# A two-layer hybrid trunk on one core: the projection tiles of a head pair are spread differently over its twelve slots

## The chip, the cores and the metric

The kernel runs on one core of a Trainium2 chip. The metric is the device time of one launch in microseconds. Three timed runs of the kernel before gave 2581.28, 2585.04 and 2586.94 us, so the median is 2585.04 us.

## The reference

The reference is a trunk of two layers over 256 context tokens and 512 latent tokens, with a model width of 1024. Each layer modulates a normalised input with a shift and a scale that come from a conditioning vector, runs a mixer, and then runs a squared-ReLU feed-forward block. The mixer of layer 0 is a gated delta rule, and that of layer 1 is retention. Only layer 0's mixer is touched by the change:

```python
proj = concat([hc, hl]) @ w_in                  # q, k, v, gate z, and the decays
qkv  = silu(short_conv(qkv, conv_w))
q, k = l2norm(q) * d ** -0.5, l2norm(k)
g, beta = -exp(a_log) * softplus(a + dt_bias), sigmoid(b)
o = bidirectional_prefix_scan(q, k, v, g, beta, n_ctx)   # chunks, both directions
y = (rmsnorm(o, norm_g) * silu(z)) @ w_out
```

Within a chunk the scan solves a unit triangular system made of `k k^T`, the decays and `beta`; from chunk to chunk it carries a state of 128 by 128 per head:

```python
sol = triangular_solve(a + eye, rhs)
un  = u - w @ s
o   = qd @ s + qk @ un
s   = s * gt + kd^T @ un
```

The modulation vectors come from `silu(c) @ w_mod + b_mod` for the latent and the context vector.

## The kernel before

Layer 0's mixer has 16 value heads in 8 pairs; the two heads of a pair share one query and one key head. Tokens are cut into 6 chunks of 128. `layer0_mix` (L289) first normalises the tokens, then prepares pair 0, and then enters a loop over pairs `p` and, in each pair, over twelve slots `n`. What runs in a slot is written out by hand:

- **The chain.** Each slot calls `gdn_step` (L826) once: six chunks, two directions in turn. A step multiplies the state by key and query (L847, L848), lets VectorE form the right-hand side `r` (L851), multiplies it by the inverse (L865), lets ACT scale and copy the result (L870, L873), updates the state (L875, L882) and forms the output (L886, L892). The step of one direction needs the state that the last step of that direction left.
- **The projection tiles.** A tile is one `conv_tile` (L572) or `z_tile` (L437). It loads 128 columns of the input weight in two halves (SP's queue, L72), splits each half into a high and a low part (ACT L56, VectorE L57), and runs two groups of 24 matmuls in L91: `gl` for the latent tokens (512 columns) and `gc` for the context (256 columns). Both land in PSUM under one tag with two buffers. A conv tile is emptied by an ACT copy (L579) and three VectorE passes per group (L582), and then gets its SiLU on ACT (L592 key, L595 query, L629 value). A gate tile is emptied by ACT alone (L442) and is stored to DRAM (L443). A pair has five tiles: key and query for pair `p + 2` (generator `g1`, from `gdn_s1`, whose third step forms the norms, L604), two value tiles for pair `p + 1` (`gv`, from `gdn_sv`), and one gate tile (`fill_z`).
- **The decays.** `gdn_bt` (L632) loads rows of cumulative decay and runs 24 ReLUs (L649) and 24 exponentials (L657) on ACT. `gdn_s2` (L661) multiplies them on VectorE with key-key and key-query products from TensorE (L670; L673, L679, L682), transposes blocks (L691), sends small blocks through DRAM (L695, L705), and runs 60 short VectorE instructions of a substitution on them (L717, L720).
- **The inverse.** `gdn_iv` (L725) sends the result through DRAM (L734, L742, L743), transposes blocks (L745, L747) and puts the inverse of each chunk together in steps of small matmuls with evictions between them (L754 to L805).
- **Modulation rows.** `mod_rows` (L220) computes 128 columns of a later modulation vector: two loads on SP's queue (L224, L226), matmuls into a PSUM buffer with the tag `py` (L232), four VectorE adds (L236) and a store (L237). The same tag serves the key and value transposes that a chain starts with (`gdn_kn`, L809, at slots 9 and 10 of the pair before; L816, L822).

The framework's scheduler turns this into one order per engine. Work in a `high_priority` block is treated as if it stood that many instructions earlier: the chain 300 (`PRI`), decays, substitution, inverse and outputs 400 (`P2`), key and query tiles 250 (`PS`). Value and gate tiles and modulation rows have no such block, so they stand where the loop puts them and fill what the rest leaves. On the chip every engine follows its order, and an instruction that waits holds up those behind it on its engine.

After the loop the remaining gate tiles run, then the output projection (`out0`), the feed-forward block, layer 1 and its feed-forward block.

Of the kernel before, what the change touches and what calls it, by code (L numbers as in the profile page):

```python
# [29 lines left out]
PRI = 300  # L30
PS = 250
P2 = 400
ZN = (6,)
GATE = 4
G3 = {11: 4}
SC0 = (3, 4)
# [6 lines left out]
class Trunk:  # L43
# [245 lines left out]
    def layer0_mix(self):  # L289
        nc = self.nc  # L290
        es_a = ExitStack()
        es_b = ExitStack()
        self.psg = self.pool(es_a, "psg", space=PSUM)
        self.gc = ("gl", 2)
        psk = self.pool(es_a, "psk", space=PSUM)
        self.wraw = self.pool(es_a, "wraw0", bufs=2)
        self.whl = self.pool(es_a, "whl0", bufs=3)
        keep = self.pool(es_a, "keep")
        with ExitStack() as es:
            npool = self.pool(es, "n0", bufs=2)  # L300
            mpool = self.pool(es, "m0")
            wpool = self.pool(es, "m1")
            col = self.mod_start(mpool, psk, "kk0")
            raw = mpool.tile([128, 8, T], F32, name="xraw")

            def x_tile(t):
                x = npool.tile([128, D], F32, tag="x0", name="x0", bufs=3)
                nc.sync.dma_start(out=x, in_=self.src_x(t))
                r, xn = self.norm_stat(npool, x)
                nc.vector.tensor_scalar(out=xn, in0=x, scalar1=r, scalar2=None, op0=ALU.mult)  # L310
                for half in range(2):
                    ps = psk.tile([128, 4, 128], F32, tag=("uo0", "uo1")[half], name="nps")
                    for k in range(4):
                        nc.tensor.transpose(ps[:, k, :], xn[:, (half * 4 + k) * 128:(half * 4 + k + 1) * 128], self.ident)
                    dst = raw[:, half * 4:half * 4 + 4, t * 128:(t + 1) * 128]
                    if half:
                        nc.scalar.activation(out=dst, in_=ps, func=AF.Copy)
                    else:
                        nc.vector.tensor_copy(dst, ps)

            mods = self.mod_cols(wpool, psk, ("kk0", "kk1"), col, raw)
            for ts in ORDER0:
                next(mods)
                for t in ts:
                    x_tile(t)
            for _ in mods:
                pass
        self.gdn_globals(keep, psk)
        self.gdn_buffers(keep)
        scan = self.pool(es_a, "scan")  # L330
        prep = self.pool(es_b, "prep")
        self.yd = self.dram.tile([16, 128, T], F32, name="yd")
        self.zd = self.dram.tile([16, 128, T], F32, name="zd")
        zs = iter(range(16))

        def fill_z():
            h = next(zs, None)
            if h is not None:
                self.z_tile(h, prep)

        st = [{} for _ in range(8)]
        self.mark = {}
        free = ("kk0", "kk1", "uo0", "uo1")
        s1 = [self.gdn_s1(p, st[p], psk, scan, prep) for p in range(8)]
        sv = [self.gdn_sv(p, st[p], prep) for p in range(8)]
        s2 = [self.gdn_s2(p, st[p], psk, scan, prep, free if p == 0 else ("pp",) if p == 1 else ("kk0", "kk1", "uo0")) for p in range(8)]
        hi = lambda: self.tc.high_priority(PRI)
        for _ in s1[0]:
            pass
        self.gdn_bt(0, st[0], prep)  # L350
        n = 0
        while True:
            with hi():
                if next(s2[0], 0) == 0:
                    for _ in self.gdn_iv(0, st[0], psk, prep, free):
                        pass
                    self.gdn_kn(0, st[0], psk, scan)
                    self.gdn_kn(1, st[0], psk, scan)
                    self.gdn_bt(1, st[1], prep)
                    break  # L360
            if n == 0:
                fill_z()
            if n in (5, 6):
                next(sv[0])
            elif 7 <= n < 10:
                next(s1[1], None)
            elif n >= 12 and n % 2 == 0 and n < 26:
                fill_z()
            n += 1
        es_l = ExitStack()  # L370

        mods = [
            self.mod_rows(prep, psk, "py", 0, ch, q) for ch in (2, 3, 4) for q in range(8)]
        mods = itertools.chain(*mods)
        ys = []
        for p in range(8):
            g1 = s1[p + 2] if p < 6 else iter(())
            gv = sv[p + 1] if p < 7 else iter(())
            g2 = s2[p + 1] if p < 7 else iter(())
            for n in range(12):  # L380
                with hi():
                    self.gdn_step(p, n // 2, n % 2, st[p], psk, scan)
                with self.tc.high_priority(P2):
                    if n == 1:
                        self.gdn_kn(2, st[p], psk, scan)
                    while ys and ys[0][0] <= 12 * p + n:
                        _, q, k = ys.pop(0)
                        self.gdn_y2(q, k, st[q], psk, self.mark["DVE"])
                    for k, last in enumerate((1, 4, 5)):
                        if n == 2 * last + 1:  # L390
                            self.gdn_y(p, k, st[p], psk, scan, scan)
                            ys.append((12 * p + n + YD, p, k))
                    for _ in range(4 if n < GATE else 0):
                        next(g2, None)
                    if n == GATE and p < 7:
                        for _ in g2:
                            pass
                        for _ in self.gdn_iv(p + 1, st[p + 1], psk, prep, gate=self.mark["ACT"]):
                            pass
                    if n in (9, 10) and p < 7:  # L400
                        self.gdn_kn(n - 9, st[p + 1], psk, scan)
                    if n in G3 and p < 6:
                        for _ in range(G3[n]):
                            next(s2[p + 2], None)
                if p < 7:
                    if n in (3, 5):
                        next(gv, None)
                    with self.tc.high_priority(PS):
                        if n in (0, 2, 4):
                            next(g1, None)  # L410
                        if n == 6 and p < 6:
                            self.gdn_bt(p + 2, st[p + 2], prep)
                    if n in ZN or (n == 9 and p == 6):
                        fill_z()
                    if n in (4, 5, 6) or n == 3 and p < 4:
                        next(mods, None)
                elif n == 1:
                    es_b.close()
                    prep = self.pool(es_l, "last")
                elif n % 3 == 0:  # L420
                    fill_z()
        with hi():
            for _, q, k in ys:
                self.gdn_y2(q, k, st[q], psk, None)
        for _ in range(16):
            fill_z()
        es_l.close()
        self.es_gdn = es_a
# [949 lines left out]
```

## Time and profile before

| | us |
|---|---|
| median of three runs | 2585.04 |
| the profiled execution | 2573.84 |
| its span, first to last instruction | 2572.1 |
| TensorE busy in the span | 2431.1 |
| chains of pairs 0 to 7, from the first step at about 188 to about | 932 |
| end of pair 0, 1, 2, 3 | 256, 373, 486, 583 |
| end of pair 4, 5, 6, 7 | 685, 785, 873, 932 |

A pair ends where the last output matmul of its chain (L886) starts. The profile is one execution with a time for every instruction. In a timeline row stand the start, the length, the engine, the line, the operation, output and inputs, the count, and in brackets the idle time of that engine just before, with the instruction that ended it. TensorE's weight loads (PEld) overlap its matmuls (PE). The granted clock is the share of TensorE's full speed; 1.00 is full speed. A matmul with float32 operands leaves two records.

### The profile page before, as it was taken

The page shows a single profiled execution, that of the slowest core. Times are in us where ns is not written, and L with a number is a line of the kernel's source. Part 1 is how long each engine was busy: PE and PEld are TensorE (multiplying, and loading weights), DVE is VectorE, ACT ScalarE, POOL GpSimd, SP SyncE. Part 2 cuts the span into 40 slices and gives each one's busy share as a digit, 9 for nine tenths or more (in the row PEclk, how much of TensorE's full clock was granted, in tenths as well). Part 3 has the DMA queues.
Part 4 walks back from the last instruction along what each step waited for, and adds up shares of the span by engine and source line. Part 5 has one row for each costly group of instructions (what it writes and reads, how often), then busy time and mean ns, then how long its engine had stood idle before and what let it go on. Part 6 is the DMA issues. An engine that isn't in the chain of part 4 may idle for free.

```text
span 2572.1 us, 39043 instructions
## 1 busy us (share of the span) xinstructions
PE 2431.1 (95%) x14879; PEld 2008.7 (78%) x14879; DVE 1667.7 (65%) x3362; ACT 1073.5 (42%) x2357; POOL 221.7 (9%) x268
## 2 busy tenths in 40 slices
PE   8799798998898999999999998999999999999998
PEld 4687686786777788778888887878888887788887
DVE  5568767787776755887776668874353546644446
ACT  5575555574555553253222221653231322532222
POOL 1102111111101110200000002000000002000001
PEclk9899899999899999999999999999999999999999
DMA  6332423423232247354443444243132223432332
GB/s 214 89 96 73 110 63 97 113 72 101 69 87 72 73 145 229 122 180 127 139 143 119 130 132 124 84 134 94 50 83 61 78 66 113 148 100 90 107 90 90
DMA packets 346827, 276.94 MB, mean 108 GB/s; under 512 B 105608, under 2 KB 293488, under 8 KB 346640
## 3 DMA queue, kind: packets, MB, share of 16 engines
q1 hardware_dynamic: 345616, 271.30, 35.4%
q10 hardware_dynamic: 1024, 3.15, 0.5%
q8 instruction: 117, 1.92, 0.3%
q14 instruction: 70, 0.57, 0.1%
HBM read 241.72 MB, written 32.67 MB: 107 GB/s over the span
## 4 chain that ended last, share of the span: by engine, by line
PE 55%; DVE 7%; DMA 3%; issue 2%; ACT 2%; POOL 0%; SPq 0%; POOLq 0%; ACTq 0%; DVEq 0%
PE pn L940 21%; PE gl L91 13%; PE rvp L1257 5%; PE gc L91 3%; PE rl L91 3%; PE rgp L1257 3%; PE pv L1287 2%; PE sc L1265 1%; DVE hl L57 1%; DVE ma L199 1%; PE rc L91 1%; DMA mraw<-in_w_mod 1%; ACT hl L56 0%; DVE o0acc L976 0%; DMA raw<-in_gdn_w_out 0%
## 5 line engine op out<-in xcount | busy, mean ns | idle before, releaser
L91 PE MATMUL gl<-xt,hl 128*128 128x512 f32 (+2 forms) x2760 | 700.8, 403 | 51.7 <-DVE acc L582 31.6
L91 PEld LDWEIGHTS gl<-xt,hl 128*128 128x128 f32 x2760 | 514.9, 193 | 160.0 <-issue 27.3
L57 DVE TENSOR_TENSOR hl<-raw,hl 128x1024 fp32r<-128x1024 f32 (+1 forms) x306 | 329.2, 1078 | 226.7 <-ACT hl L56 225.6
L940 PE MATMUL pn<-hl,fh 128*128 128x512 f32 x1920 | 445.0, 391 | 2.0 <-DVE fh L1074 1.9
L56 ACT ACTIVATE hl<-raw 128x1024 fp32r<-128x1024 f32 (+1 forms) x306 | 280.1, 920 | 396.9 <-PE pn L940 263.0
L940 PEld LDWEIGHTS pn<-hl,fh 128*128 128x128 f32 x1920 | 357.1, 188 | 80.1 <-DVE fh L1074 5.1
L91 PE MATMUL gc<-xt,hl 128*128 128x256 f32 x1944 | 274.8, 290 | 9.4 <-DVE acc L582 4.7
L91 PEld LDWEIGHTS gc<-xt,hl 128*128 128x128 f32 x1944 | 254.4, 194 | 20.6 <-ACT zs L442 5.4
L199 DVE SCALAR_TENSOR_TENSOR ma<-mraw,cst,ma 128x256 f32<-128x256 f32 x280 | 127.6, 496 | 40.0 <-DMA mraw<-in_w_mod 37.7
L940 PE MATMUL pn<-hl,yh 128*128 128x512 f32 x576 | 137.4, 397 | 5.4 <-DVE yh L57 4.1
L954 DVE TENSOR_TENSOR facc<-pn,facc 128x512 f32<-128x512 f32 x120 | 82.5, 689 | 83.1 <-PE pn L940 82.7
L1257 PE MATMUL rvp<-hl,xt 128*128 128x512 f32 x576 | 133.3, 390 | 0.6 <-DVE hl L57 0.6
L940 PEld LDWEIGHTS pn<-hl,yh 128*128 128x128 f32 x576 | 108.4, 191 | 31.2 <-DVE yh L57 5.8
L1257 PEld LDWEIGHTS rvp<-hl,xt 128*128 128x128 f32 x576 | 107.7, 188 | 23.5 <-DVE hl L57 1.1
L1071 ACT ACTIVATE fr<-gl 128x512 f32<-128x512 f32 x64 | 38.2, 597 | 202.1 <-PE gl L91 202.1
L582 DVE SCALAR_TENSOR_TENSOR acc<-gl,cw,acc 128x511 f32<-128x511 f32 (+1 forms) x96 | 71.5, 745 | 39.3 <-ACT acc L579 38.5
L977 POOL TENSOR_TENSOR facc<-facc,rx 128x1024 f32<-128x1024 f32 x10 | 26.5, 2645 | 781.1 <-DVE facc L976 478.8
L940 PE MATMUL pn<-hl,ryt 128*128 128x512 f32 x384 | 91.7, 396 | 0.0
L1257 PE MATMUL rgp<-hl,xt 128*128 128x512 f32 x384 | 91.3, 393 | 0.0
L91 PE MATMUL rl<-xt,hl 128*128 128x512 f32 x384 | 89.5, 391 | 0.4 <-DVE hl L57 0.4
L717 DVE TENSOR_TENSOR tmp<-u 112x30 f32<-112x30 f32 (+14 forms) x240 | 81.3, 339 | 9.2 <-POOL u L709 6.0
L940 PEld LDWEIGHTS pn<-hl,ryt 128*128 128x128 f32 x384 | 71.5, 187 | 17.0
(282 smaller groups left out, 3437.0 us busy)
## 6 DMA issues: line engine op xcount, KB each, us to landing
raw<-in_w_ff SPq DMA_DIRECT2D x128, 512.0 KB
mraw<-in_w_mod SPq DMA_DIRECT2D x112, 256.0 KB
raw<-in_gdn_w_in SPq DMA_DIRECT2D x96, 256.0 KB
raw<-in_ret_w_in SPq DMA_DIRECT2D x32, 512.0 KB
mraw<-in_w_mod SPq DMA_DIRECT2D x24, 512.0 KB
e<-gd SPq DMA_DIRECT2D x32, 384.0 KB
mraw<-in_w_mod SPq DMA_DIRECT2D x8, 1024.0 KB
raw<-in_gdn_w_out SPq DMA_DIRECT2D x16, 512.0 KB
```

Source lines behind the costliest of these rows:

```text
L56: nc.scalar.activation(out=hi, in_=src, func=AF.Copy)
L57: nc.vector.tensor_tensor(out=lo, in0=src, in1=hi.bitcast(F32), op=ALU.subtract)
L91: nc.tensor.matmul(ps, lhsT=w(a, k), rhs=xt[:, b, k, t0:t0 + n], start=(k == 0 and i == 0), stop=(k == 7 and i == 2))
L199: eng.scalar_tensor_tensor(out=accs[v], in0=raw[:, k], scalar=c, in1=accs[v], op0=ALU.mult, op1=ALU.add)
L582: nc.vector.scalar_tensor_tensor(out=acc[:, t0 + a:t0 + a + m], in0=ps[:, b:b + m], scalar=c[j], in1=acc[:, t0 + a:t0 + a + m], op0=ALU.mu ...
L717: nc.vector.tensor_tensor(out=t3, in0=u3[:, 0:c, c:c + 1].to_broadcast([112, c, n]), in1=u3[:, c:c + 1, c + 1:32].to_broadcast([112, c, n] ...
L940: m = nc.tensor.matmul(ps, lhsT=lhs(a, k, t), rhs=hls[hf][k // 2][:, b, k % 2], start=(k == 0 and n == 0), stop=(k == 3 and n == 2))
L954: nc.vector.tensor_tensor(out=dst, in0=ps, in1=dst, op=ALU.add)
L977: nc.gpsimd.tensor_tensor(out=a, in0=a, in1=x, op=ALU.add)
L1071: nc.scalar.activation(out=r, in_=ps, func=AF.Relu)
L1257: nc.tensor.matmul(ps, lhsT=xt[:, a, kk, t * 128:(t + 1) * 128], rhs=hls[kk // 2][:, b, kk % 2], start=(kk == 0 and n == 0), stop=(kk == 7 ...
L1287: nc.tensor.matmul(pvs[it], lhsT=pts[jt][:, i, it * 128:(it + 1) * 128], rhs=v[:, j, jt], start=(jt == 0 and n == 0), stop=(jt == 5 and n ...
```

## The change

The slots of a pair are dealt out differently. The two value tiles move from slots 3 and 5 to 4 and 6. The gate tile moves from slot 6 to 10. The modulation rows move from slots 4, 5 and 6 to 5, 7 and 8; the one at slot 3 in the first four pairs stays. Key and query tiles (slots 0 and 2), norms (slot 4), decays (slot 6), the second gate tile of pair 6 (slot 9), the chain and its priorities stay.

```diff
-ZN = (6,)
+ZN = (10,)
...
                 if p < 7:
-                    if n in (3, 5):
+                    if n in (4, 6):
                         next(gv, None)
                     with self.tc.high_priority(PS):
                         if n in (0, 2, 4):
                             next(g1, None)
                         if n == 6 and p < 6:
                             self.gdn_bt(p + 2, st[p + 2], prep)
                     if n in ZN or (n == 9 and p == 6):
                         fill_z()
-                    if n in (4, 5, 6) or n == 3 and p < 4:
+                    if n in (5, 7, 8) or n == 3 and p < 4:
                         next(mods, None)
```

The scheduler answers with another order on every engine. Three places of it, first boundary between pairs on TensorE, the second on ACT, and the one between pairs 4 and 5 on TensorE, are shown in the prediction.

## The prediction

> **What bounds the kernel now.** The page comes first. TensorE is busy nearly all the time, so a pure change of order can win only where TensorE waits.
>
> ```profile
> span 2572.1 us, 39043 instructions
> PE 2431.1 (95%) x14879; PEld 2008.7 (78%) x14879; DVE 1667.7 (65%) x3362; ACT 1073.5 (42%) x2357; POOL 221.7 (9%) x268
> ```
>
> The change concerns the pair loop alone. Second view: busy time by stretch. Seven stretches run from the last step of one pair's chain to the first steps of the next (I call them seams 1 to 7, seam 1 lying between pairs 0 and 1); the last row is the loop from seam 1 to the end of pair 7. Columns: length, then PE, PEld, DVE, ACT, POOL busy, then the granted clock, the share and the GB/s of DMA.
>
> ```profile
> 256.00:320.00 64.00, 50.99 (x589) 42.82 (x590) 48.00 (x113) 33.99 (x85) 7.84 (x14) 0.84 0.40 106
> 373.00:427.00 54.00, 43.81 (x287) 36.73 (x287) 36.80 (x85) 31.27 (x76) 8.17 (x14) 0.94 0.42 115
> 484.00:530.00 46.00, 40.25 (x318) 33.55 (x315) 35.06 (x86) 21.45 (x62) 6.49 (x9) 1.00 0.44 123
> 575.00:628.00 53.00, 41.50 (x349) 34.43 (x337) 39.01 (x93) 25.00 (x62) 7.19 (x10) 0.90 0.41 108
> 684.00:723.00 39.00, 26.54 (x190) 21.00 (x187) 31.33 (x78) 15.69 (x38) 5.47 (x8) 0.87 0.45 119
> 785.00:830.00 45.00, 36.77 (x247) 30.27 (x245) 30.98 (x73) 22.97 (x49) 8.52 (x15) 0.92 0.34 89
> 866.00:900.00 34.00, 33.62 (x512) 27.24 (x511) 19.71 (x45) 15.96 (x42) 2.57 (x3) 1.00 0.31 86
> 256.00:932.00 676.00, 602.80 (x5749) 501.42 (x5749) 497.22 (x1297) 387.14 (x1115) 102.27 (x147) 0.95 0.31 83
> ```
>
> Length less PE gives the idle time: 13.0, 10.2, 5.75, 11.5, 12.5, 8.2 and 0.4 us, 61.5 of the loop's 73.2. So the chains are packed and the seams are not. Third view, who TensorE waited for from 256 to 940 us (total, times, longest):
>
> ```profile
> PE gl L91 <- DVE acc L582: 23.9, 6, 9.1
> PE gl L91 <- DVE hl L57: 6.8, 4, 3.1
> PE ivps L754 <- DVE v L745: 6.0, 1, 6.0
> PE gl L91 <- ACT hl L56: 4.7, 2, 4.3
> PE mps L232 <- DVE mrow L236: 3.9, 1, 3.9
> ```
>
> Projection tiles share two PSUM banks (tag gl, two buffers), and a value tile frees a bank only after an ACT copy (L579) and three VectorE passes (L582). At a seam ACT also owes 24 exponentials (L657) and VectorE the decay products (L673 to L682) for the next pair. Seam 2 shows the queueing: the copy stood behind all 24.
>
> ```profile
> 382.94 7.13 ACT L657 ACTIVATE e<-e,lw 128x128 f32<-128x128 f32 x24
> 385.13 3.03 PE L91 MATMUL gc<-xt,hl 128*128 128x256 f32 x24
> 388.10 0.62 PE L232 MATMUL mps<-mraw,cst 128*2 128x128 f32 x16
> 390.09 1.28 ACT L629 ACT_TABLE_LOAD   x1
> 392.13 0.67 ACT L579 ACTIVATE acc<-gl,cw 128x512 f32<-128x512 f32 x1
> 397.78 4.76 PE L91 MATMUL gl<-xt,hl 128*128 128x512 f32 x14 [9.06 <-DVE acc L582]
> ```
>
> **The change part by part.** Nothing is added to or taken from the arithmetic: five tiles and three or four modulation rows per pair, as before. The one new instruction is an activation table load (45 against 44 in the order), on ACT, which is busy 16 to 34 of the 39 to 64 us of a seam; other ACT idle time hides it, and I cost it at nothing; without that cover it costs its own 1.3 us (the row at 390.09 above). What changes is which work meets which seam.
>
> Seam 1. Before, TensorE ran out of tiles while the inverse's blocks made their trip through DRAM; then the inverse ran bare and at a slow clock.
>
> ```profile
> 257.20 1.50 PE L604 MATMUL ssps<-ones,sq 128*128 128x1 f32 x12
> 261.31 5.78 PE L91 MATMUL gl<-xt,hl 128*128 128x512 f32 x24
> 273.94 1.56 PE L754 MATMUL ivps<-v,off 32*32 32x32 f32 x92 [5.95 <-DVE v L745]
> 276.08 1.63 PE L762 MATMUL ivps<-pc,tt 32*32 32x32 f32 x48 [0.58 <-ACT pc L757]
> 278.86 1.50 PE L769 MATMUL ivps<-tt,pc 32*32 32x32 f32 x96 [1.16 <-DVE v L765]
> 280.29 4.99 PE L91 MATMUL gc<-xt,hl 128*128 128x256 f32 x24
> 290.97 1.25 PE L797 MATMUL ivps<-tt,pc 64*64 64x64 f32 x24 [1.37 <-DVE tt L805]
> 311.02 0.74 PE L91 MATMUL gc<-xt,hl 128*128 128x256 f32 x4 [3.18 <-ACT zs L442]
> 352.05 0.97 PE L754 MATMUL ivps<-v,off 32*32 32x32 f32 x90
> 353.83 0.95 PE L762 MATMUL ivps<-pc,tt 32*32 32x32 f32 x48
> 356.52 1.01 PE L769 MATMUL ivps<-tt,pc 32*32 32x32 f32 x96
> ```
>
> TensorE's order there, before, from the last chain matmul of pair 0 (L886) to the first of the inverse (L754); gl and gc are the two halves of a tile, ssps the norms, mps a modulation row:
>
> ```order
> L886 MATMUL uo_3094<-un,qkd_598 128x128 x2
> L91 MATMUL gc<-xt,hl 128x256 x5
> L604 MATMUL ssps<-ones,sq 128x1 x6
> L91 MATMUL gc<-xt,hl 128x256 x17
> L232 MATMUL mps_2661<-mraw,cst 2x128 x8
> L91 MATMUL gl<-xt,hl 128x512 x24
> L232 MATMUL mps_2771<-mraw,cst 2x128 x8
> L754 MATMUL ivps<-v_605,off_1977 32x32
> ```
>
> The same stretch as it stands now:
>
> ```order
> L886 MATMUL uo_3094<-un,qkd_598 128x128 x2
> L91 MATMUL gl<-xt,hl 128x512 x16
> L91 MATMUL gc<-xt,hl 128x256 x22
> L604 MATMUL ssps<-ones,sq 128x1 x12
> L91 MATMUL gl<-xt,hl 128x512 x3
> L754 MATMUL ivps<-v_605,off_1977 32x32
> L91 MATMUL gl<-xt,hl 128x512
> L232 MATMUL mps_2683<-mraw,cst 2x128 x8
> L91 MATMUL gl<-xt,hl 128x512 x8
> L754 MATMUL ivps<-v_2354,off_1977 32x32
> L91 MATMUL gl<-xt,hl 128x512 x12
> ```
>
> A tile now covers the trip. At 0.24 us a gl (5.78/24), 0.126 a gc (3.03/24), 0.62 a modulation row and 1.5 for six norms (12 records), the cover was 22 gc, 24 gl, 6 norms and two rows, 11.3 us; now 40 gl, 27 gc (five follow the rows shown), 12 norms and one row, 16.6. Of the 5.95 us some 0.7 stays. The slow clock cost 3.7: 0.6 on L754, 0.7 on L762, 0.5 on L769, 1.9 on the 24 gc. The Trainium skill, "TensorE: Matmul & The Clock Gate", Part 1 (the HAM clock gate), says that an idle window of about 3.4 us halves the clock and that as long a busy one restores it. The halving agrees with these rows; an estimate from that page, 3.4 us at half pace, would be a loss of 1.7 us, and by it the sum would be 2 us poorer. Against the gain stand new costs, each an estimate from a row: half of the bare waits between inverse steps (0.58, 1.16, 1.37 and small ones, 3.9 in all) 1.9; a run of nine exponentials ahead of an eviction, 9 x 0.30 less cover, 2.0; the value tile's copy, still behind 24 exponentials, 2.3 and a weight split 2.0 (both as at seam 5 below). 8.9 against 13.0 + 3.7 = 16.7: a gain of 7.8.
>
> Seam 2. ACT's order before, from the table load ahead of the exponentials:
>
> ```order
> L657 ACT_TABLE_LOAD
> L657 ACTIVATE e_4023<-e_4023,lw 128x128 x12
> L657 ACTIVATE e_4038<-e_4038,lw 128x128 x12
> L629 ACT_TABLE_LOAD
> L629 ACTIVATE vt<-acc 128x768
> L579 ACTIVATE acc<-gl,cw 128x512
> ```
>
> Nothing but a value tile's last activation follows the 24 before the copy. ACT's order now has them in the last steps of the chain ahead of that seam, between the evictions of the inverse (L757, L764):
>
> ```order
> L657 ACT_TABLE_LOAD
> L657 ACTIVATE e_4005<-e_4005,lw 128x128 x7
> L757 ACTIVATE pc<-ivps 128x384
> L657 ACTIVATE e_4005<-e_4005,lw 128x128 x4
> L764 ACTIVATE v_605<-ivps_3628 32x12x32
> L657 ACTIVATE e_4005<-e_4005,lw 128x128
> L901 ACTIVATE y,ms<-o 128x128 x2
> ```
>
> The exponentials are moved into the chain, where before they already lay for seams 3, 4 and 5; the value tile's copy no longer waits for them, only its VectorE passes for the decay products. Seams 3 and 4 bound that at 5.75 and 11.5; I take the mean, 8.6, for every seam of this kind. Seam 2 was 10.2 + 1.4 (14 gl in 4.76 instead of 3.4), so it gains 3.0; seam 3, of this kind before and after, moves from 5.75 to 8.6, a loss of 2.85; seam 6 moves from 8.2 to 8.6, a loss of 0.4. Seam 4 becomes the kind in which all 24 exponentials stand ahead of the copy: the mean of seams 2 and 6, 9.2, and 2.3 for a query tile that is now finished before the chain starts. That is what such a tile waited at seam 4 for its passes among the substitution steps (L717, L720), against 11.5: nothing.
>
> ```profile
> 619.53 0.70 PE L91 MATMUL gl<-xt,hl 128*128 128x512 f32 x2 [2.34 <-DVE acc L582]
> ```
>
> Seam 5 had four separate stalls:
>
> ```profile
> 694.58 1.04 PE L232 MATMUL mps<-mraw,cst 128*2 128x128 f32 x16 [3.91 <-DVE mrow L236]
> 697.59 4.12 PE L91 MATMUL gl<-xt,hl 128*128 128x512 f32 x10 [1.97 <-DVE hl L57]
> 705.19 2.97 PE L91 MATMUL gl<-xt,hl 128*128 128x512 f32 x12 [2.30 <-DVE acc L582]
> 709.19 0.93 SPq L72 DMA_DIRECT2D raw<-in_gdn_w_in  x2
> 714.42 1.07 PE L91 MATMUL gl<-xt,hl 128*128 128x512 f32 x2 [4.28 <-ACT hl L56]
> ```
>
> TensorE's order there, before:
>
> ```order
> L91 MATMUL gc<-xt,hl 128x256 x13
> L232 MATMUL mps_7577<-mraw,cst 2x128 x8
> L91 MATMUL gl<-xt,hl 128x512 x10
> L91 MATMUL gc<-xt,hl 128x256 x10
> L91 MATMUL gl<-xt,hl 128x512 x12
> ```
>
> Little more than two tiles stood there. Now the stretch reads, from the second modulation row on:
>
> ```order
> L232 MATMUL mps_7723<-mraw,cst 2x128 x8
> L91 MATMUL gl<-xt,hl 128x512 x6
> L91 MATMUL gc<-xt,hl 128x256 x6
> L91 MATMUL gl<-xt,hl 128x512 x24
> L91 MATMUL gc<-xt,hl 128x256 x25
> L91 MATMUL gl<-xt,hl 128x512 x24
> L91 MATMUL gc<-xt,hl 128x256 x29
> L91 MATMUL gl<-xt,hl 128x512 x2
> ```
>
> Gate, key and query tiles now stand here in a row, and their weight loads are no longer queued on SP behind a modulation row's store (the 4.28). I put the seam at 8.6 + 2.3 = 10.9: a gain of 1.6. Seam 7 loses cover: between the inverse's steps of pair 7 fewer tiles are left. Bare, those waits were 3.9 at seam 1; half covered they are 2.0, a loss of 2.0. One tile more runs after pair 7, where nothing waits for it but the same TensorE.
>
> Sum: -7.8 - 3.0 + 2.85 + 0 - 1.6 + 0.4 + 2.0 = -7.2. The profiled execution took 2573.84 us, 1.7 more than its span, and the median of the runs is 2585.04, 0.4% above it. The forecast is 2566.6 in the one's time, 2577.8 in the other's.
>
> **The rivals.** A, slower: VectorE's queue holds all releases at once. The passes of a tile, the low halves of the next weights (L57) and the adds of the modulation rows (L236) all stand among or behind the decay products, and the moved rows at 7 and 8 bring both adds to that place. Then seams 2, 3, 5 and 6 would each cost what seam 5 did, 12.5: 50.0 instead of 3 x 8.6 + 10.9 = 36.7, which turns -7.2 into +6.1, 2591. It makes the change slower than nothing from 11 us a seam on. For it: all four stalls of seam 5 are of this sort, and VectorE is busy 31.3 of its 39 us. Against it: seam 3, with the same sequence, cost 5.75.
>
> B, much faster: seams 2, 3, 5 and 6 come out like seam 3 (2.85 less each, -11.4), together -18.6, 2566. If besides seam 1 stays at full clock and what it lost is read from its column (0.16 x 64 = 10.2) and not from rows (3.7), 6.5 more, 2560. By the rule of the Trainium skill, "TensorE: Matmul & The Clock Gate", Part 1, waits under 3.4 us would not slow the clock. For B: seam 3 ran at a clock of 1.00. Against it: it wants the best of the seams four times.
>
> C, no change: the loop is set by the recurrence exponentials, products, substitution, DRAM trip, inverse, not by tiles, and waits only move: 2585. For it: pairs differ in idle time, yet VectorE works 497 of 676 us. Against it: TensorE works 603.
>
> **How the numbers follow.** About 0.2%, 5 us, is what a measurement can tell from no change. The forecast gets 0.42, with errors of some 8 us about it (2570 to 2586), so a quarter of it lies within 5 us of no change; A 0.27, B 0.17, C 0.14. Faster: 0.31 + 0.17 = 0.48; same: 0.11 + 0.14 = 0.25; slower 0.27. The range reaches from a little beyond B's lower value, 2557, to A with the slow clock of seam 5 (0.13 x 39 = 5.1) and as much again, 2600.
>
> **What would show it.** Right: at seam 1 the wait for L745 is under 1.5 us and the clock above 0.95; at seam 2 no wait near 9; seam 4 has one instead; seam 7 shows waits of 2 us. Wrong: waits on L236, L57 or L582 that add up to over 11 us at seams 2, 5 and 6, or chain stretches that lose more than the 11.7 us they lose now because exponentials delay ACT's evictions.

## The result, and the profile after

The change made the kernel slower. Six runs of the changed kernel gave a median of 2601.72 us (2599.15 to 2606.14), six of the kernel before 2583.63 us (2578.61 to 2586.94) on the same chip: a ratio of 1.0074, interval 1.0059 to 1.0089, so 18 us. The forecast was 2577.8 us. The profiled executions, 2573.84 and 2606.14 us, lie further apart than the medians: the one of before was faster than any of its six timed runs, and the two kernels ran 5 us apart before the first chain step, where their orders are the same.

Page of the changed kernel: span, and busy time with the number of instructions.

```profile
span 2604.4 us, 39057 instructions
PE 2447.7 (94%) x14879; PEld 2017.1 (77%) x14879; DVE 1670.7 (64%) x3362; ACT 1075.6 (41%) x2358; POOL 219.5 (8%) x268
```

TensorE ran the same 14879 matmul records as before. So the 32.3 us by which the spans differ split exactly: TensorE was idle 156.7 us (2604.4 less 2447.7) against 141.0, 15.7 more, and busy 16.6 us longer with the same work. Most of the second part is a slower clock, as its records show below. 1.6 us of the idle and 3.6 us of the busy time lie before the first chain step, where the order is the same, so they are not the change's.

Busy time by stretch, changed kernel: the seven seams, cut as in the prediction, then the loop (columns: length, PE, PEld, DVE, ACT, POOL, granted clock, DMA share, GB/s).

```profile
258.00:341.00 83.00, 66.96 (x673) 55.53 (x672) 57.86 (x137) 41.02 (x96) 8.36 (x14) 0.88 0.38 98
399.00:442.00 43.00, 36.50 (x225) 30.30 (x224) 32.12 (x78) 21.95 (x60) 5.48 (x8) 0.96 0.48 132
493.00:541.00 48.00, 40.99 (x297) 33.76 (x298) 37.96 (x91) 22.64 (x58) 5.71 (x8) 0.93 0.45 118
588.00:664.00 76.00, 61.03 (x357) 50.85 (x356) 50.02 (x120) 38.96 (x95) 8.37 (x15) 0.89 0.33 92
718.00:773.00 55.00, 42.80 (x250) 35.94 (x249) 40.34 (x99) 24.22 (x61) 5.48 (x8) 0.91 0.40 108
827.00:859.00 32.00, 27.09 (x175) 21.62 (x174) 25.58 (x64) 12.65 (x33) 5.48 (x8) 0.95 0.43 111
891.00:925.00 34.00, 32.14 (x506) 26.11 (x506) 19.79 (x44) 16.43 (x49) 3.01 (x4) 1.00 0.20 53
258.00:953.00 695.00, 610.31 (x5731) 501.24 (x5730) 501.03 (x1309) 388.12 (x1114) 100.57 (x147) 0.95 0.30 80
```

Length less PE: the seams are idle for 16.0, 6.5, 7.0, 15.0, 12.2, 4.9 and 1.9 us, 63.5 in all (61.5 before); the loop for 84.7 (73.2 before), so the chains between the seams for 21.2 (11.7 before). The clock column is below 0.97 at six seams, before at five. The loop's busy time compares less directly: 20 gl and 24 gc more than before now run after it.

Who TensorE waited for, changed kernel, from 258 to 960 us (total, times, longest):

```profile
PE gl L91 <- DVE acc L582: 21.4, 6, 7.1
PE gc L91 <- DVE acc L582: 18.5, 7, 4.8
PE yps L921 <- DVE o L915: 8.6, 9, 1.4
PE gc L91 <- ACT zs L442: 6.1, 5, 2.0
PE ivps L784 <- DVE tt L776: 3.8, 2, 3.6
PE mps L232 <- DVE mrow L236: 3.6, 1, 3.6
...
PE gl L91 <- DVE hl L57: 2.2, 2, 1.4
```

The waits on weight splits by ACT (4.7) have gone, those on L745 fell from 6.0 to 1.0 and those on L57 from 6.8 to 2.2. The second row grew most: the context half of a tile, gc, waits for a bank that VectorE's passes hold; before, from 256 to 940 us, that was one wait of 4.2 us. The third row, the output transposes, was 6.7 us. TensorE at seams 1, 4, 5 and 6 of the changed kernel:

```profile
288.03 1.54 PE L784 MATMUL ivps<-v,off 64*64 64x64 f32 x24 [3.64 <-DVE tt L776]
290.15 1.55 PE L784 MATMUL ivps<-v,off 64*64 64x64 f32 x24 [0.58 <-ACT pc L790]
...
305.98 0.62 PE L232 MATMUL mps<-mraw,cst 128*2 128x128 f32 x16 [3.62 <-DVE mrow L236]
...
331.92 2.26 PE L91 MATMUL gc<-xt,hl 128*128 128x256 f32 x9 [4.76 <-DVE acc L582]
...
648.88 4.55 PE L91 MATMUL gc<-xt,hl 128*128 128x256 f32 x24 [3.75 <-DVE acc L582]
...
656.02 0.47 PE L91 MATMUL gc<-xt,hl 128*128 128x256 f32 x2 [2.12 <-DVE acc L582]
...
725.43 3.42 PE L91 MATMUL gl<-xt,hl 128*128 128x512 f32 x14 [3.42 <-DVE acc L582]
...
833.35 4.92 PE L91 MATMUL gl<-xt,hl 128*128 128x512 f32 x14 [2.21 <-DVE acc L582]
```

ACT and then VectorE around the wait that ends at 648.88:

```profile
644.67 0.67 ACT L579 ACTIVATE acc<-gl,cw 128x512 f32<-128x512 f32 x1
```

```profile
645.78 0.36 DVE L720 TENSOR_TENSOR u<-u,tmp 112x220 f32<-112x220 f32 x1
646.08 0.73 DVE L582 SCALAR_TENSOR_TENSOR acc<-gl,cw,acc 128x510 f32<-128x510 f32 x1
646.73 0.37 DVE L717 TENSOR_TENSOR tmp<-u 112x228 f32<-112x228 f32 x1
647.04 0.73 DVE L582 SCALAR_TENSOR_TENSOR acc<-gl,cw,acc 128x511 f32<-128x511 f32 x1
647.70 0.37 DVE L720 TENSOR_TENSOR u<-u,tmp 112x228 f32<-112x228 f32 x1
648.00 0.73 DVE L582 SCALAR_TENSOR_TENSOR acc<-gl,cw,acc 128x511 f32<-128x511 f32 x1
```

Two things are to be seen. The copy ends at 645.34, the first pass starts 0.74 us later, and the three passes alternate with substitution steps, so that 2.2 us of passes take until 648.73. The gc matmuls are next in TensorE's order, so it stands still meanwhile. And behind most waits the matmuls are slow: 24 gc in 4.55 instead of 3.0, 14 gl in 4.92 instead of 3.4, 24 L784 of the inverse in 1.54 instead of the 0.92 that the same row takes at 285.21 in the kernel before. Not behind all: the rows at 656.02 and 725.43 run at full pace after waits of 2.12 and 3.42 us.

The trace records the granted clock, which puts a number on this. In all twenty traces of this study it is either 1.00 or 0.50, and it changes only on a grid of 3.41 us, whose place against the kernel's start differs from one execution to the next. Around the row at 833.35 (columns as above):

```profile
829.66:833.07 3.41, 1.48 (x24) 1.04 (x23) 3.41 (x7) 1.15 (x3) 0.00 (x0) 1.00 0.17 47
833.07:836.48 3.41, 3.13 (x7) 2.49 (x8) 3.41 (x8) 0.00 (x0) 1.56 (x2) 0.50 0.50 129
836.48:839.89 3.41, 3.41 (x22) 2.95 (x20) 3.29 (x8) 0.85 (x1) 2.49 (x5) 1.00 0.41 64
```

From the first chain step to the end of pair 7, before has 9 spells at 0.50 and the changed kernel 14. Their sums, before and changed:

```profile
sum 61.46, PE 42.74 PEld 35.99 DVE 49.39 ACT 14.47 POOL 15.09; mean PE 4.75 PEld 4.00 DVE 5.49 ACT 1.61 POOL 1.68
sum 68.27, PE 58.07 PEld 48.64 DVE 52.53 ACT 19.07 POOL 14.56; mean PE 4.15 PEld 3.47 DVE 3.75 ACT 1.36 POOL 1.04
```

As an estimate, half of TensorE's busy time in such spells is lost to the clock: 21.4 us before and 29.0 in the changed kernel, 7.7 more. Over the whole span the busy time at 0.50 went from 69.0 to 98.2 us, and half of the difference is 14.6 of the 16.6 us; 4.7 of it lies before the first chain step and 2.2 behind the loop.

### The profile page after: what moved, and what is told of

The parts are those of the page before. It is cut to its first block, busy times and chain, and to the rows that moved or that the text cites. A ratio compares the mean times of both kernels' runs of the same rounds, so it can differ in the third digit from the quotient of the medians.

```text
span 2604.4 us, 39057 instructions
## 1 busy us (share of the span) xinstructions
PE 2447.7 (94%) x14879; PEld 2017.1 (77%) x14879; DVE 1670.7 (64%) x3362; ACT 1075.6 (41%) x2358; POOL 219.5 (8%) x268
## 4 chain that ended last, share of the span: by engine, by line
PE 72%; DVE 13%; ACT 4%; issue 3%; DMA 2%; POOL 1%; SPq 0%; POOLq 0%; ACTq 0%; DVEq 0%
PE pn L940 22%; PE gl L91 18%; PE gc L91 6%; PE rvp L1257 5%; PE rl L91 3%; PE rgp L1257 3%; PE pv L1287 2%; DVE hl L57 1%; DVE acc L582 1%; PE sc L1265 1%; PE kk L875 1%; PE uo L865 1%; PE uo L886 1%; DVE tmp L717 1%; PE kk L847 1%
## 5 line engine op out<-in xcount | busy, mean ns | idle before, releaser
L57 DVE TENSOR_TENSOR hl<-raw,hl 128x1024 fp32r<-128x1024 f32 (+1 forms) x306 | 328.7, 1076 | 212.0 <-ACT hl L56 210.7
L56 ACT ACTIVATE hl<-raw 128x1024 fp32r<-128x1024 f32 (+1 forms) x306 | 280.9, 921 | 421.7 <-PE pn L940 278.7
L91 PE MATMUL gc<-xt,hl 128*128 128x256 f32 x1944 | 274.6, 291 | 26.3 <-DVE acc L582 20.1
L91 PEld LDWEIGHTS gc<-xt,hl 128*128 128x128 f32 x1944 | 256.5, 196 | 38.0 <-issue 21.4
L582 DVE SCALAR_TENSOR_TENSOR acc<-gl,cw,acc 128x511 f32<-128x511 f32 (+1 forms) x96 | 71.3, 743 | 52.3 <-ACT acc L579 51.8
```

What stands on the lines that cost most here:

```text
L56: nc.scalar.activation(out=hi, in_=src, func=AF.Copy)
L57: nc.vector.tensor_tensor(out=lo, in0=src, in1=hi.bitcast(F32), op=ALU.subtract)
L91: nc.tensor.matmul(ps, lhsT=w(a, k), rhs=xt[:, b, k, t0:t0 + n], start=(k == 0 and i == 0), stop=(k == 7 and i == 2))
L582: nc.vector.scalar_tensor_tensor(out=acc[:, t0 + a:t0 + a + m], in0=ps[:, b:b + m], scalar=c[j], in1=acc[:, t0 + a:t0 + a + m], op0=ALU.mu ...
```

## Experiments

In the table below, "idle" and "busy" are TensorE's, from the page of each kernel, as differences to before's 141.0 and 2431.1 us; the last three columns are its waits from 190 to 1000 us. Ratio and interval are against runs of the kernel before on the same chip, whose medians were between 2577.16 and 2586.67 us. Idle and busy show one execution of each kernel, and that of before took less time than the median, so the two together exceed the loss that the ratio shows: by 14 us in the second row. The kernels ran on several chips, and the change itself cost 18 us when first measured and 28.8 the second time, so differences of some 10 us between rows of different chips tell nothing.

| kernel | ratio (95%) | idle | busy | gc on L582 | mps on L236 | gl on L56 |
|---|---|---|---|---|---|---|
| before | 1 | 0 | 0 | 4.7 | 3.9 | 4.7 |
| changed | 1.0074 (1.0059 to 1.0089) | +15.7 | +16.6 | 20.1 | 3.6 | 0.0 |
| changed, second time | 1.0109 (1.0094 to 1.0124) | +13.9 | +18.8 | 20.1 | 3.6 | 0.0 |
| rows only | 1.0257 (1.0237 to 1.0276) | +27.5 | +41.0 | 42.3 | 1.2 | 4.9 |
| values only | 1.0136 (1.0120 to 1.0153) | +21.9 | +12.3 | 2.9 | 17.1 | 7.6 |
| gate only | 1.0158 (1.0142 to 1.0173) | +18.0 | +31.2 | 9.1 | 7.9 | 13.3 |
| changed, rows back | 1.0146 (1.0132 to 1.0160) | +17.6 | +21.3 | 2.0 | 17.0 | 14.0 |
| pair 0 only | 1.0001 (0.9988 to 1.0013) | -6.9 | +6.9 | 8.9 | 6.3 | 0.3 |
| pair 1 only | 1.0099 (1.0081 to 1.0117) | +21.2 | +11.8 | 12.2 | 2.4 | 0.0 |
| pairs 1, 2 | 1.0066 (1.0048 to 1.0084) | +13.1 | +10.6 | 14.5 | 0.0 | 0.0 |
| pairs 0 to 2 | 1.0058 (1.0042 to 1.0073) | +11.3 | +8.6 | 20.3 | 3.6 | 0.0 |
| pairs 3, 4 | 1.0002 (0.9990 to 1.0015) | +3.4 | +3.4 | 8.0 | 0.3 | 1.0 |
| pairs 5, 6 | 1.0011 (0.9999 to 1.0024) | +9.0 | +4.1 | 4.7 | 3.9 | 1.6 |
| pairs 3 to 6 | 0.9989 (0.9979 to 0.9999) | +3.1 | +0.3 | 13.0 | 0.3 | 0.0 |
| all but pairs 1, 2 | 1.0123 (1.0108 to 1.0138) | +20.8 | +12.7 | 20.3 | 9.5 | 1.6 |
| changed, late query tile | 1.0052 (1.0034 to 1.0071) | +16.4 | +3.5 | 11.9 | 5.5 | 2.0 |
| changed, rows in pp | 1.0091 (1.0071 to 1.0111) | +4.1 | +27.1 | 30.1 | 0.0 | 0.0 |
| before, rows in pp | 1.0047 (1.0031 to 1.0063) | +2.3 | +15.8 | 13.9 | 0.0 | 2.8 |
| changed, wide norms | 1.0035 (1.0022 to 1.0049) | +5.6 | +9.7 | 13.6 | 3.1 | 1.0 |
| before, wide norms | 1.0159 (1.0139 to 1.0179) | +20.3 | +27.3 | 8.1 | 2.7 | 2.4 |

**One part at a time.** My first theory, Q, came from the rows above: at seams 1, 4 and 5 the order now puts a whole query tile ahead of the next chain, and its gc half waits for VectorE. I blamed the modulation rows, which share a PSUM buffer with the chain's first transposes.

```diff
-                    if n in (4, 5, 6) or n == 3 and p < 4:
+                    if n in (5, 7, 8) or n == 3 and p < 4:
```

> Before with one part of the change: the modulation rows at slots 5, 7, 8; value and gate tiles where they were. Theory Q (the moved rows hold the PSUM buffer that the next chain starts with, so the order puts the whole query tile, its context half and the tile after it ahead of the chain; each of these groups waits 2 to 5 us for VectorE's passes over the one before): here the query tile stands whole ahead of the chain of pairs 1 to 5, so this part alone is slower than before by as much as the whole change or more, 15 to 30 us, and TensorE's waits of gc groups for L582 come to 15 us or more (4 before, 18.5 after). Rival G (the gate tile at slot 10 takes cover from the seams, and the rows are harmless): within 5 us of before. Rival C (the parts add up, each a third): 4 to 8 us slower.

```diff
-                    if n in (3, 5):
+                    if n in (4, 6):
```

> Before with one part: value tiles at slots 4 and 6. Theory Q: no query tile ahead of the chain anywhere, so no gc waits of the after kind (under 6 us in all) and a time within 8 us of before, either way. Rival G: within 5 us of before. Rival V (a value tile at slot 6 is what lacks its evictions, behind the decays of the same slot): slower by 10 us or more. Rival C: 4 to 8 us slower.

```diff
-ZN = (6,)
+ZN = (10,)
```

> Before with one part: the gate tile at slot 10. Theory Q: the query tile is only half ahead of the chain in pairs 1, 3 and 5, so at most half the loss of the change: 0 to 9 us slower, gc waits for L582 under 10 us. Rival G: all of the loss, 14 to 22 us slower, with the waits of TensorE at the inverse steps of pairs 6 and 7. Rival C: 4 to 8 us slower.

The changed kernel with one part undone:

```diff
-                    if n in (5, 7, 8) or n == 3 and p < 4:
+                    if n in (4, 5, 6) or n == 3 and p < 4:
```

> The changed kernel with the modulation rows back at slots 4, 5, 6 (values at 4 and 6, gate at 10). Theory Q: no query tile is whole ahead of a chain (all chains start after at most 14 of the context matmuls that follow it), gc waits for L582 fall from 18.5 to under 8 us, and of the 18 us at least 12 come back: within 6 us of before. Rival G and rival V: the loss stays, 12 to 20 us slower than before. Rival C: about 12 us slower.

Every part alone is slower than the three together: 67, 36 and 42 us above before (medians 2644.30, 2613.38 and 2619.18 against 2577.16), where the whole costs 18 (28.8 when measured again). All three times miss the ranges of theory Q, by 28 us and more. Undoing one part did not help either: 2615.76, 39 us. The waits of the rows-only kernel, largest two, and of the kernel with the rows put back:

```profile
PE gc L91 <- DVE acc L582: 42.3, 17, 4.1
PE gl L91 <- DVE acc L582: 12.9, 6, 4.6
```

```profile
PE mps L232 <- DVE mrow L236: 17.0, 7, 4.1
PE gl L91 <- ACT hl L56: 14.0, 2, 7.5
...
PE gc L91 <- DVE acc L582: 2.0, 2, 1.6
```

Theory Q is right on what the moved rows do: with them the gc waits come to 20.1 and 42.3 us, without them to 2.0, 2.9 and 9.1. It is wrong on the time: with the rows back other waits are as large, for the adds of the rows and for weight splits. The rivals that put the loss on one part, or a third on each, fall too; rival V's 10 us or more came for the values alone, but the other parts cost as much.

**One place at a time.** The next runs give the new slots to some pairs only. For pair 0:

```diff
-                    if n in (3, 5):
+                    if n in ((4, 6) if p in (0, 99) else (3, 5)):
...
-                    if n in ZN or (n == 9 and p == 6):
+                    if n in ((10,) if p in (0, 99) else ZN) or (n == 9 and p == 6):
...
-                    if n in (4, 5, 6) or n == 3 and p < 4:
+                    if n in ((5, 7, 8) if p in (0, 99) else (4, 5, 6)) or n == 3 and p < 4:
```

> Before, with the new slots in pair 0 alone; TensorE's order at seam 1 is then the changed kernel's up to the start of pair 1's chain, and that of pairs 6 and 7 is before's. Theory L (the loss sits at the places where the query tile stands whole ahead of the chain, and each place costs what it cost in the changed kernel): pair 1 is about 12 us longer than before beyond its extra tiles, the gc wait near 4.8 us for L582 is there again, and the kernel is 6 to 16 us slower. Rival N (the loss has no place: any other order than before's meets new waits somewhere, and the clock doubles them): 15 to 40 us slower, with waits spread over pairs 1 to 5. Rival S (seam 1 gains, as predicted, and the loss is made later): 0 to 8 us faster.

The same with `(3, 4)` and with `(5, 6)`:

> Before, with the new slots in pairs 3 and 4 alone; pairs 1 and 2 keep before's order, the query tile stands whole ahead of the chains of pairs 4 and 5. Theory L: gc waits for L582 of 2 to 4 us each at the seams 4 and 5, 8 us or more in all, and 8 to 20 us slower (13 from the pairs 4 and 5 of the changed kernel beyond their tiles). Rival N: 15 to 40 us slower, waits in pairs 6 and 7 too. Rival S: the same as the theory here.

> Before, with the new slots in pairs 5 and 6 alone; pairs 1 to 5 keep before's order, pairs 6 and 7 are within a few tiles of the changed kernel's, whose pair 6 was 4.8 us shorter than before's beyond its tiles. Theory L: no query tile is left for those chains, so nothing is lost: 0 to 8 us faster than before. Rival N: 5 to 20 us slower.

And the changed kernel with the query tile put behind the chain's start:

```diff
-                    with self.tc.high_priority(PS):
+                    with self.tc.high_priority(100 if n == 2 else PS):
                         if n in (0, 2, 4):
```

> The changed kernel with the query tile's priority lowered from 250 to 100, so that it stands behind the start of the next chain except at seam 3. Theory L: the gc waits for L582 fall from 20 us to under 8 and the time comes back to 0 to 8 us above before. Rival N: gc waits fall too, but waits of another name (L236, L57, L56, L582 of gl) take their place and the time stays 15 us or more above before.

Pair 0, pairs 3 and 4 and pairs 5 and 6 each cost nothing that can be told (1.0001, 1.0002, 1.0011), although the first has 8.9 and the second 8.0 us of gc waits. Theory L, which priced each such place, is refuted: pairs 3 and 4 were to cost 8 to 20 us. Rival N, by which any other order costs 15 us or more (5 for pairs 5 and 6), is refuted by the same runs. The page of the pair-0 kernel:

```profile
span 2572.1 us, 39040 instructions
PE 2438.0 (95%) x14879; PEld 2012.7 (78%) x14879; DVE 1663.9 (65%) x3362; ACT 1074.6 (42%) x2358; POOL 222.6 (9%) x268
```

6.9 us less idle, 6.9 us more busy: in this execution waits were traded for busy time, of which 2.9 us lie in the loop. But it was the fastest of its kernel's twelve, 13.5 us below their median, so it doesn't show why the medians agree. The late query tile brought the gc waits down from 20.1 to 11.9 us, not below 8, and 12 us of loss stayed, between the ranges of L and N: its waits have other names, gl on L582 the largest with 28.9.

**Halves, and another buffer.** Slots changed in pairs 0 to 2, then in pairs 3 to 6, as above:

> Before, with the new slots in pairs 0, 1 and 2; TensorE's order is the changed kernel's up to seam 3. Theory A (the loss is a sum over pairs of what each lost in the changed kernel's profile: waits plus slow clock, beyond its tiles, +6 in pair 1, -1 in pair 2, +6 in pair 3): 6 to 14 us slower than before. Rival K (the new slots cost nothing while before's slots follow, as in the runs with pairs 0, 3 and 4, or 5 and 6 alone; the loss needs the new slots in all pairs, whose tiles pile up to the last): within 5 us of before. Rival N (any other order costs 15 us or more): 15 to 40 us slower.

> Before, with the new slots in pairs 3 to 6, the other half of the change. Theory A: +9 and +3 in pairs 4 and 5, -5 in pair 6, so 2 to 12 us slower than before. Rival K: within 5 us of before. Rival N: 15 to 40 us slower.

And the modulation rows moved to the buffer of the decay products, in the changed kernel and in the one before:

```diff
-            self.mod_rows(prep, psk, "py", 0, ch, q) for ch in (2, 3, 4) for q in range(8)]
+            self.mod_rows(prep, psk, "pp", 0, ch, q) for ch in (2, 3, 4) for q in range(8)]
```

> The changed kernel with the modulation rows in the PSUM buffer of the decay products (pp) instead of that of the chain's first transposes (py); the order then starts each chain with 0 to 24 gl matmuls ahead of it instead of 22 to 114. Theory P (the moved rows hold the buffer, so the tiles go ahead of the chain and wait for VectorE): gc waits for L582 fall from 20 us to under 8 and the time is 8 us or more below the changed kernel's, within 8 us of before. Rival D (the buffer isn't what the chain waits for; the inverse and the decay products, which now share a buffer with the rows, are): chains wait for rows instead (L236 ahead of kkps or ivps), and the time stays 15 us or more above before.

> The kernel before with the same move of the rows from buffer py to pp, slots as before. Theory P: the wait of mps for L236 (3.9 us) and the tiles ahead of the chain go, 2 to 15 us faster than before. Rival D: decay products and inverse wait for the rows, 5 to 30 us slower.

The halves look like a sum: +14.6 and -2.0 us make 12.6, where the whole cost 18 or 28.8. But theory A wanted 2 to 12 us from the second half, and there rival K came true; the first half is just above A's 14. The buffer is a miss for theory P: the order starts each chain with fewer tiles ahead, the rows' own waits on L236 are gone (rival D's waits ahead of the inverse come to 1.4 us), idle is only 4.1 us above before, and the time is still 23.6 us above. Almost all of it is busy time: 27.1 us, of which 25.7 are the clock by the estimate of half the busy time at 0.50. Its gc waits rose to 30.1 us, twelve of the fifteen between 1 and 3 us. Moving the rows made before slower too (1.0047), by 12.8 us: rival D's range, without the waits that it named.

**Is it a sum, and what makes the clock slow?** The changed kernel again, with no edit:

> The changed kernel unchanged, for a second profile. Theory W (waits and slow clock share the loss): 13 to 23 us slower than before; TensorE idle 10 us or more above before's 141.0 and busy 8 us or more above its 2431.1, with the same number of matmuls. Rival O (the slow clock of the first profile was chance): idle as in the first profile, busy within 4 us of before's.

```profile
PE 2449.9 (94%) x14879; PEld 2020.5 (78%) x14879; DVE 1671.4 (64%) x3362; ACT 1074.7 (41%) x2358; POOL 220.0 (8%) x268
```

With a span of 2604.8 us idle is 154.9: both shares are within 2.2 us of the first profile's. Theory W holds on both shares, and rival O falls. The time is outside W's range: 28.8 us above before on this chip, where 13 to 23 were expected. The single slow spell, however, is chance. The rows of seams 5 and 6 in this second profile, where the first had 725.43 and 833.35:

```profile
726.81 5.46 PE L91 MATMUL gl<-xt,hl 128*128 128x512 f32 x12 [3.41 <-DVE acc L582]
...
835.33 3.44 PE L91 MATMUL gl<-xt,hl 128*128 128x512 f32 x14 [2.21 <-DVE acc L582]
```

It is the same kernel with the same waits: after 2.21 us the clock was 0.50 in the first execution and 1.00 in the second, after 3.4 us the other way round. Of 13 waits of 2 us or more in the loop, 10 met a slow clock in the first and 11 in the second, and three of the 13 differ. What differs is how the wait lies on the grid. In the two cases that ended in a slow clock, the wait left TensorE busy for 1.48 us (829.66 to 833.07, first execution) and 1.41 us (721.98 to 725.39, second) of one stretch of 3.41 us. In the other two it fell across two stretches, with 1.58 and 1.82 us busy in the first execution and 1.91 and 2.70 in the second.

Pairs 1 and 2, then all the others, then pair 1 alone:

> Before, with the new slots in pairs 1 and 2. Theory A (the loss lies in pairs 1 and 2, pair 0 being neutral by itself): 9 to 18 us slower than before. Rival I (it needs pair 0 as well: a gate tile put off in three pairs in a row sets how the tiles meet the later chain starts): within 5 us of before.

> The change everywhere but in pairs 1 and 2. Theory A (the loss lies in pairs 1 and 2 and the rest adds 0 and -3): 8 us faster to 3 us slower than before. Rival M (there is no such place: each mix of slots is an order of its own, and most orders wait more than before's): 8 us or more slower, waits of another set of seams.

> Before, with the new slots in pair 1 alone. TensorE's order of pairs 4 to 7 is then that of the runs with pairs 0 to 2 and 1 and 2 (15 and 16 us slower), though their slots are before's. Theory A with its place in pair 1's own boundary, seam 2: 6 to 12 us slower, the waits at seam 2. Theory T (the loss is made in the tiles' phase later on, at the seams 3 to 5): 8 to 18 us slower with the waits at seams 3, 4 and 5. Rival P2 (it is pair 2's slots): within 4 us of before.

Pairs 1 and 2 cost 16.2 us, as theory A wanted. But all other pairs together cost 31.6, where theory A wanted 3 at most, although pair 0 and pairs 3 to 6 are free when changed apart. So the loss isn't a sum over pairs. Pair 1 alone costs 27.2 us, above every range given for it; against the 16.2 of pairs 1 and 2, measured on another chip, that is not clear of such differences. Its waits of 2 us and more behind seam 2 stand at seams 3 to 6, so theory T was nearest on the place. Rival M is what is left: each mix is an order of its own, with its own waits.

The last two kernels give each norm matmul 32 equal columns instead of one, so that TensorE's array has more work in it:

```diff
...
-        ps = psk.tile([128, 2, NCH], F32, tag="py", name="ssps")
+        ps = psk.tile([128, 2, NCH, 32], F32, tag="py", name="ssps")
...
-                        ps[:, a, hf * 3 + c:hf * 3 + c + 1], lhsT=sq[:, c, a], rhs=self.ones[:, 0:1],
+                        ps[:, a, hf * 3 + c], lhsT=sq[:, c, a], rhs=self.ones[:, 0:32],
...
```

> The changed kernel with 32 equal columns for each norm matmul instead of one (the first is read), so TensorE's array works longer in each; the order shifts by some tiles. Theory N (twelve one-column matmuls within 4 us count as idle for the clock): no slow rows without a wait right behind L604 any more (6.3 us of them in the changed kernel), busy 4 us or more below the changed kernel's 2447.7. Rival F (they aren't the cause): slow rows still follow L604, in at least two of the six pairs.

> The kernel before with the same 32 columns. Theory N: no slow rows without a wait behind L604 (3.2 us in pair 4 before), 0 to 8 us faster. Rival F: slow rows still follow L604 in one or two pairs; by the new order alone up to 30 us slower, as the other orders were.

TensorE in the kernel before, in pair 4, with no wait anywhere:

```profile
656.49 1.40 PE L604 MATMUL ssps<-ones,sq 128*128 128x1 f32 x12
657.75 0.68 PE L847 MATMUL kk<-s,kq 128*128 128x256 f32 x2
...
658.91 1.68 PE L604 MATMUL ssps<-ones,sq 128*128 128x1 f32 x12
660.45 0.78 PE L865 MATMUL uo<-r,tt 128*128 128x128 f32 x2
...
662.47 2.71 PE L91 MATMUL gc<-xt,hl 128*128 128x256 f32 x11
```

Nearly the same stretch of the changed kernel with wide norms:

```profile
682.55 1.42 PE L604 MATMUL ssps<-ones,sq 128*128 128x32 f32 x12
683.81 0.68 PE L847 MATMUL kk<-s,kq 128*128 128x256 f32 x2
...
684.96 1.30 PE L604 MATMUL ssps<-ones,sq 128*128 128x32 f32 x10
...
686.61 0.69 PE L865 MATMUL uo<-r,tt 128*128 128x128 f32 x4
```

Behind one-column norms two L865 records take 0.78 us, behind wide ones four take 0.69. In the changed kernel with wide norms no norm is followed by slow rows without a wait in any of the six pairs, its busy time is 6.9 us lower, and it is 9.5 us above before: as theory N expected. It doesn't prove N, since narrow norms often meet no slow clock either: in the eighteen other traces 28 of 108 sets of norms in the loop do so without a wait, in pairs 3 and 4 and in pairs 5 and 6 none of six, and the set at 594 us of the changed kernel did in its first execution but not in its second. In the kernel before with wide norms it failed in one pair, where the norms alternate with matmuls of 64 by 64:

```profile
583.81 0.41 PE L604 MATMUL ssps<-ones,sq 128*128 128x32 f32 x2
584.15 0.32 PE L784 MATMUL ivps<-v,off 64*64 64x64 f32 x2
584.40 0.62 PE L604 MATMUL ssps<-ones,sq 128*128 128x32 f32 x2
584.96 0.47 PE L784 MATMUL ivps<-v,off 64*64 64x64 f32 x2
```

Here TensorE is busy without a gap and still becomes half again as slow in the middle of a run of small matmuls; the clock's record changes to 0.50 at 584.45. That kernel is 41 us slower than before, outside the ranges of N and F, with 20.3 us more idle. So narrow matmuls alone can be followed by a slow clock. Whether widening them helps isn't shown, since both edits moved the order as well.

No version beat the kernel before by more than can be told: the best, the new slots in pairs 3 to 6, is at 0.9989. Not tried: an edit that removes a wait and leaves the order as it is, since every edit of a cost moves the scheduler's whole order.

## Why the prediction was wrong, point by point

The step that failed is the one that made the sum: it priced waits at the seams alone, took the slow clock for something that only goes away (3.7 us at seam 1 and 1.4 at seam 2), and gave the chains between the seams no term. In idle time alone the forecast was -7.2 + 5.1 = -2.1 us. The runs showed +2.0 us of idle at the seams, +9.5 in the chains and +7.7 of slow clock in the loop (an estimate from the clock's records). In its own terms:

- **Seam 1, "the slow clock cost 3.7", gain 7.8.** The trip was covered as forecast: waits on L745 fell from 6.0 to 1.0 us. But 8.9 us of new costs became 16.0 of idle. The inverse's waits, estimated at 1.9 in all, came to 4.9 (3.64, 0.58, 0.66); the row's wait (3.62) and the gc wait (4.76) had no term of their own. And the slow clock stayed: TensorE was busy at 0.50 for 15.7 us there before and for 17.5 after, column 0.88 where I named 0.95 as the mark. Half of the 15.7 is 7.8, so the 3.7 that I read from four rows was also too small for what the clock cost.
- **Seam 2, gain 3.0.** Right in kind and better in size: the copy no longer stands behind 24 exponentials, no wait is near 9 (3.4 the longest), idle 6.5 against my 8.6.
- **Seams 3, 5, 6 and 7.** 7.0, 12.2, 4.9 and 1.9 us against my 8.6, 10.9, 8.6 and 2.4: near enough, 4.5 better in all.
- **Seam 4, no change.** The wait behind the exponentials came, 7.1, and the query tile had two waits, 3.75 and 2.12, where I had one of 2.3. Idle 15.0 against 11.5. The query tile's price was read from one row, 619.53, and used as if such a tile met one wait.
- **The chains, no term.** I named a loss of more than their 11.7 us as a sign of failure. They went to 21.2. Not because of exponentials ahead of evictions, as I had it: the rows are waits of output transposes (7.8, was 5.5), of inverse steps that now run bare inside the chain (L754 to L797, 5.5, was 0.6) and of the steps themselves.
- **The clock, no term for new waits.** 21.4 to 29.0 us by the estimate: +7.7 where I had -5.1. This error, 12.8 us, is as large as the one in idle time, 13.6 (+11.5 in the loop against -2.1).
- **Rival A** had the right sign with the wrong mechanism. Its waits (L236, L57, L582 at seams 2, 5 and 6) add up to 18.9 us, over my mark of 11, but the same sum before was 25.3: the mark couldn't tell the two apart. **Rival B**'s condition, seams that keep the clock up because waits are short, is refuted at seam 5: behind the wait of 2.01 us that ends at 763.84 the clock was 0.50 from 764.80, and behind the same wait (2.12) in the second profile too. By the Trainium skill, "TensorE: Matmul & The Clock Gate", Part 1 (the HAM clock gate), an idle window of about 3.4 us slows the clock; here it also slowed after a window in which TensorE was busy for 1.48 of 3.41 us (829.66 to 833.07), so the threshold as I used it does not hold. The section on psum-queue depth-cycling of the same page of the Trainium skill, where many short idle spells between groups cost throughput at each return, agrees with the 14 spells, of 1.4 to 4.0 us each by the estimate. **Rival C** fell.

What stays open is why one mix of slots meets many waits and another few, and how much of the clock's share is the change's: for the same order before the first chain step, 4.7 us of it came and went between two executions. It was only argued, by theories Q, L and A, that one part, one kind of place or one pair carries it, and each of them failed on a run.

## What to carry to other kernels

Where a scheduler fits tiles between a chain, don't sum a change of order seam by seam: of eighteen other versions of this loop fourteen were slower by 0.35 to 2.6%, four were within 0.2%, and parts that were free apart cost 1.2% together. Split the loss first, idle against busy at a constant instruction count: here about half of it was clock, which no list of waits shows. And price a new wait of 2 us or more on TensorE with a chance of slow matmuls behind it: 10 of 13 such waits met a slow clock here, at an estimated 1.4 to 4.0 us for each spell. Profile a kernel twice before reading a single slow spell: three of the 13 changed sides.

## What the runs showed of the hardware that was not expected

- A wait is not needed for the slow clock. Twice twelve one-column matmuls within 4 us (656.49 to 660.59 in the kernel before) were followed by a granted clock of 0.50 from 660.00 to 666.83, and in the midst of a run of small matmuls without a gap the same two went from 0.41 to 0.62 us at 584.40. In the profile TensorE is busy all the while.
- The granted clock was 1.00 or 0.50 in all twenty traces and changed on a grid of 3.41 us that lies differently in each execution. So the same row behind the same wait of 2.21 us took 4.92 us in one execution (833.35) and 3.44 in the next (835.33).
- Less waiting can cost as much: in the changed kernel with the rows in pp TensorE was idle only 4.1 us longer than in the kernel before, and busy 27.1 us longer.
